# A staging tile of its own for the recurrence's output, and its reload in single 128-row blocks

## Chip, core and metric

One core of a Trainium2 chip runs the whole program. The metric is device microseconds of one execution; the comparison is between medians of several executions. The core has a matrix engine (TensorE), VectorE, ScalarE, GpSimd, the sync engine SP, and 16 DMA engines that all queues share. In the profile they are PE (with PEld for its weight loads), DVE, ACT, POOL and SP; a "q" behind a name (SPq, ACTq) is an instruction of that engine's sequencer, such as the issue of a DMA.

## What is computed

One layer of a hybrid decoder for 1024 tokens of width 1024, in float32. The input is normed and projected by one large matrix; one part of the columns goes to dilated sliding-window attention, one to the RWKV-7 recurrence, one to the gates:

```python
h = rmsnorm(x, norm_mix_pre)
f_att, f_rwkv, f_gate = split(h @ w_in)
o_att  = dilated_window_attention(...)                  # 3 groups, 12 heads
o_rwkv = rwkv7_time_mix(token_shift(f_rwkv), ...)       # 16 heads of 64
gates  = sigmoid(f_gate + b_gate)
merged = gates[0] * (o_att @ w_att_branch) + gates[1] * (o_rwkv @ w_rwkv_branch)
x = x + rmsnorm(merged @ w_out, norm_mix_post)
h = rmsnorm(x, norm_ffn_pre)
x = x + rmsnorm(square(relu(h @ w_ffn1)) @ w_ffn2, norm_ffn_post)
```

The change lies in the recurrence. For every head a 64 x 64 state goes through the tokens; its output y is normed per head, scaled and shifted, given a bonus term and a gate:

```python
state = state*decay + outer(state @ -kk, kk*a) + outer(v, k);  y_t = state @ r_t
y = (y - mean(y)) * rsqrt(var(y) + eps) * ln_w + ln_b
o_rwkv = (y + sum(r*k*r_k) * v) * g           # g = sigmoid(fg) @ w_g2
```

## The kernel before, in words

Every dense product takes both operands in two parts (hi and lo, made by `split_hi_lo`, L40: a cast on ScalarE and a subtraction on VectorE) and adds three matmuls (`mm3`, L203; lines L209, L211, L213). Weights come through a ring of raw tiles (`Weights`, L152). After the input norm, `Project` makes the recurrence's operands and writes them to HBM; attention follows, with the inverses of the chunk matrices beside it; then comes the stage of this change, and after it the merge, the output projection and the feed-forward part.

The recurrence (`Chain`, L817) takes the 1024 tokens in 16 chunks of 64. For each chunk `load` (L840) brings operands U, SV, TB and BKT from HBM into tiles with two buffers, SV being the state with the values. `chunk` (L858) issues five groups of 32 small matmuls, named here by their outputs and lines: pr (L874), py (L879), a second pr (L883), pst (L889), py (L896). Between them stand copies and sums: RS (L876, VectorE) after the first pr, the two halves of SV (L884 on ScalarE and L885 on VectorE) after the second, the next chunk's state (L893, VectorE) after pst, and yt (L898, ScalarE) after py. pst reads both halves of SV.

After each second chunk, a block J of 128 tokens is complete and `norm` (L901) runs on it: mean (L914 to L916, VectorE), then Square into the scratch tile y2 (L918, ScalarE), the sum over y2 (L920, VectorE), a power on GpSimd (L923), and the scaling and bonus (L924 to L926). Later `post` (L929) multiplies by the gate (matmul L937, VectorE L938) and transposes the block in two halves of four (L948, TensorE). For blocks 0 to 5 ScalarE copies the halves into a tile (L953) and issues a store of 512 KB to the HBM tensor O_d (L956). That tile is allocated under the name y2 in a pool with one buffer, so it is the norm's scratch tile again. Blocks 6 and 7 go straight to the operands of the next product (`direct`, L951).

Those operands are ohi and olo, which hold the recurrence's output for the branch projection as eight row blocks of 128 rows by 1024 tokens. They are allocated where the normed hidden states hhi and hlo lay, once the last dense step on these is issued. `load_branch` (L984) fills them from O_d through the tile orw with two buffers: one call for tokens 0 to 511, one for tokens 512 to 767 (blocks 4 and 5), each in four pieces of two row blocks. `Merge.first` (L1005) then starts the branch projection on the first 512 tokens, and on the next 256, for two output tiles, going through all eight row blocks for each.

The order of work: for TensorE and GpSimd it is the order of the program text, which `weave` (L62) makes by planned costs and due times. In this stage the main line is gate and attention branch projections (`gt.open`, `gt.branch`), and the chunks and the posts are woven in as sides. For ScalarE, VectorE and SP a scheduler orders the instructions by a simulated timeline before the program is built, with the chunks' steps at high priority. On the chip each engine, and SP's queue of DMA issues, works in its order; a wait holds up what stands behind it. The pools reuse memory, and a new tile waits until the last reader of the old one is done, a store's DMA included.

Of the kernel before, what the change touches and what calls it, by code (L numbers as in the profile page):

```python
# [9 lines left out]
F32 = mybir.dt.float32  # L10
# [29 lines left out]
def split_hi_lo(nc, raw, hi, lo):  # L40
    nc.scalar.copy(hi, raw)  # L41
    nc.vector.tensor_sub(lo, raw, hi)  # L42
# [774 lines left out]
class Chain:  # L817
# [111 lines left out]
    def post(self, J):  # L929

        g, nc, one = self.g, self.g.nc, self.one
        ts = slice(J * 128, (J + 1) * 128)
        sf, yf, ready = self.normed.pop(J)
        yield 0.0, max(0.0, ready - g.clock)
        for cs in HALF:
            pg = self.ps.tile([128, 512], F32, name="po")
            nc.tensor.matmul(pg, sf, self.wg[:, cs], start=True, stop=True)  # L937
            nc.vector.tensor_mul(yf[:, cs], yf[:, cs], pg)  # L938
            yield 858.0, 1200.0
        direct = self.direct is not None  # L940
        if not direct:
            self.split = J + 1
            oT = one.tile([128, 8, 128], F32, name="y2")
        for q in range(2):
            pt = self.ps.tile([128, 512], F32, name="po")
            for i in range(4):
                k = q * 4 + i
                nc.tensor.transpose(pt[:, i * 128:(i + 1) * 128], yf[:, k * 128:(k + 1) * 128], g.ident)  # L948
            p3, ks = pt.rearrange("p (k t) -> p k t", k=4), slice(q * 4, q * 4 + 4)
            if direct:  # L950
                split_hi_lo(nc, p3, self.direct[0][:, ks, ts], self.direct[1][:, ks, ts])  # L951
            else:
                nc.scalar.copy(oT[:, ks, :], p3)  # L953
            yield 430.0, 1500.0
        if not direct:
            nc.scalar.dma_start(g.O_d[:, :, ts], oT)  # L956
# [27 lines left out]
def load_branch(g, wk, ohi, olo, j0, j1):  # L984

    nc, ts = g.nc, slice(j0 * 128, j1 * 128)
    for q in range(4) if j1 > j0 else ():
        ks = slice(q * 2, q * 2 + 2)
        orw = wk.tile([128, 2, 512], F32, name="orw")[:, :, 0:(j1 - j0) * 128]
        nc.sync.dma_start(orw, g.O_d[:, ks, ts])  # L990
        split_hi_lo(nc, orw, ohi[:, ks, ts], olo[:, ks, ts])

# [456 lines left out]
def layer(tc, ins, out):  # L1449
# [4 lines left out]
    with ExitStack() as c:  # L1454
# [46 lines left out]
        with ExitStack() as c1:  # L1501
# [39 lines left out]
            with ExitStack() as c2:  # L1541
                ch = Chain(g, ins, c2)
                run, posts = Side(ch.run(), 1.1), Side(ch.posts())
                step = lambda f, ci: f(ci, gp) if f == gt.open else f(ci, at.hi, at.lo)
                weave(g, seq(*[step(*x) for x in order[1:-2]]), rest=(run, posts))
                hs.close()
                with tc.using_default_side("left"):
                    op = pool(os, "op")
                    owk = pool(os, "owk", bufs=2)
                ohi = op.tile([128, 8, 1024], F32R, name="ohi")  # L1550
                olo = op.tile([128, 8, 1024], F32R, name="olo")
                ch.direct = (ohi, olo)
                mg = Merge(g, W, ohi, olo)
                done = ch.posted
                load_branch(g, owk, ohi, olo, 0, min(done, 4))
                load_branch(g, owk, ohi, olo, 4, done)

                def ready():
                    if ch.posted < 6:
                        return False  # L1560
                    load_branch(g, owk, ohi, olo, done, ch.split)
                    return True

                weave(g, seq(*[step(*x) for x in order[-2:]], mg.first(ready)), run, posts)
# [87 lines left out]
```

## Time and profile before

| | us |
|---|---|
| median of 3 runs | 1954.45 |
| lowest, highest | 1944.74, 1958.83 |
| the profiled execution, its own time | 1958.2 |
| its span in the profile | 1956.5 |

Mean granted TensorE clock of the profiled execution: 0.972 of full speed. Busy times over the span:

| engine | busy us | share |
|---|---|---|
| PE | 1850.8 | 95% |
| DVE | 1230.8 | 63% |
| ACT | 793.7 | 41% |
| POOL | 307.4 | 16% |

Times inside the profile are counted from the start of the span. A matmul counts as busy from its start to a modelled end, at whatever clock it runs, so a busy PE may still be slow. In timelines a bracket behind a row gives the idle time before it on that engine and what ended it. The name y stands for y2 (numbers behind names are left out), so "O_d<-y" is the store of L956.

### The profile page before, as it was taken

To read this page: it belongs to the slowest core of one execution; us is meant where nothing else is said; L and a number is where in the kernel's file an instruction comes from. 1 tells how busy PE (TensorE), PEld (TensorE's weight loads), DVE (VectorE), ACT (ScalarE), POOL (GpSimd) and SP (SyncE) were. 2 spreads that over 40 slices of the span, in tenths; PEclk is the share of its full clock that TensorE was granted. 3 is DMA by queue.
4 is the path that set the end of the run, shared out by engine and by line. 5 is a ranking of instruction groups with operands and counts; after the bars stand their busy time and mean duration, and the time that the engine had idled before them with its cause. 6 is when DMAs were issued, how large, how long until landed. Compare 5 with 4: busy or idle time off the path is not lost.

```text
span 1956.5 us, 30888 instructions
## 1 busy us (share of the span) xinstructions
PE 1850.8 (95%) x12183; PEld 1509.2 (77%) x12183; DVE 1230.8 (63%) x1857; ACT 793.7 (41%) x1379; POOL 307.4 (16%) x398
## 2 busy tenths in 40 slices
PE   8999999999999999978888899989999998999996
PEld 7888888887787887666666788767888887888885
DVE  6777777734324324436566654668777776776877
ACT  7533333323534525312222333336666655433342
POOL 2011111126141507013333300310000000000001
PEclk9999999999998999989998999999999999999998
DMA  6355556652242241399898454436454447453225
GB/s 181 92 138 139 148 151 153 153 136 69 52 141 55 69 103 40 82 240 235 209 221 208 141 197 136 148 112 229 141 162 143 153 153 241 144 187 136 87 98 182
DMA packets 324914, 283.83 MB, mean 145 GB/s; under 512 B 84926, under 2 KB 275488, under 8 KB 324384
## 3 DMA queue, kind: packets, MB, share of 16 engines
q1 hardware_dynamic: 261984, 247.76, 44.5%
q10 hardware_dynamic: 60672, 26.75, 5.1%
q0 software_dynamic: 2112, 7.34, 1.1%
q8 instruction: 96, 1.57, 0.3%
q14 instruction: 50, 0.41, 0.1%
HBM read 184.70 MB, written 96.57 MB: 144 GB/s over the span
## 4 chain that ended last, share of the span: by engine, by line
PE 76%; DMA 9%; DVE 5%; issue 4%; POOL 3%; ACT 2%; SPq 1%; ACTq 0%; DVEq 0%; POOLq 0%
PE fx L1400 16%; PE fx L1252 14%; PE pd L209 12%; PE pd L211 12%; PE pd L213 12%; DMA O_d<-y 3%; DMA SV<-V_d 2%; PE pm L460 2%; DMA U<-AK_d 1%; PE pm L430 1%; PE po L694 1%; POOL X L515 1%; SPq L501 1%; POOL tmp L514 1%; PE ppt L679 1%
## 5 line engine op out<-in xcount | busy, mean ns | idle before, releaser
L1400 PE MATMUL fx<-w2s,x 128*128 128x512 f32 (+1 forms) x1362 | 307.8, 388 | 5.9 <-DVE w2s L42 4.1
L209 PE MATMUL pd<-hhi,whi 128*128 128x512 f32 (+1 forms) x880 | 300.9, 419 | 0.4 <-DVE Q L590 0.4
L1400 PEld LDWEIGHTS fx<-w2s,x 128*128 128x128 f32 x1362 | 254.9, 189 | 59.0 <-DVE w2s L42 4.4
L211 PE MATMUL pd<-hlo,whi 128*128 128x512 f32 (+1 forms) x880 | 276.9, 392 | 1.0 <-DVE mv L125 1.0
L213 PE MATMUL pd<-hhi,wlo 128*128 128x512 f32 (+1 forms) x880 | 276.0, 391 | 0.0
L42 DVE TENSOR_TENSOR wlo<-raw,whi 128x512 fp32r<-128x512 f32 (+2 forms) x164 | 113.5, 726 | 169.9 <-ACT whi L41 167.4
L211 PEld LDWEIGHTS pd<-hlo,whi 128*128 128x128 f32 x880 | 167.6, 190 | 37.0 <-DVE mv L125 1.3
L213 PEld LDWEIGHTS pd<-hhi,wlo 128*128 128x128 f32 x880 | 167.8, 191 | 35.9
L1252 PE MATMUL fx<-xh,wop 128*128 128x512 f32 x600 | 187.7, 390 | 2.6 <-ACT e L1256 1.6
L209 PEld LDWEIGHTS pd<-hhi,whi 128*128 128x128 f32 x880 | 152.4, 191 | 33.3 <-issue 8.6
L41 ACT CAST whi<-raw 128x512 fp32r<-128x512 f32 (+2 forms) x164 | 92.2, 608 | 198.2 <-PE pd L211 147.4
L1252 PEld LDWEIGHTS fx<-xh,wop 128*128 128x128 f32 x600 | 112.6, 188 | 27.1 <-ACT e L1256 2.0
L41 ACT CAST x<-xr 128x1024 fp32r<-128x1024 f32 x56 | 59.0, 1054 | 153.2 <-issue 87.0
L1252 PE MATMUL fx<-xl,wop 128*128 128x512 f32 x300 | 116.8, 389 | 0.0
L42 DVE TENSOR_TENSOR x<-xr,x 128x1024 fp32r<-128x1024 f32 x56 | 68.4, 1222 | 62.4 <-ACT x L41 62.4
L1354 POOL TENSOR_TENSOR rs<-mv,nhalf 128x1 f32<-128x1 f32 x8 | 6.3, 789 | 629.1 <-ACT jk L1365 608.7
L1181 ACT ACTIVATE e<-e 128x512 f32<-128x512 f32 x128 | 80.2, 633 | 31.0 <-DVE e L1276 10.5
L1252 PE MATMUL fx<-mh,wop 128*128 128x512 f32 x240 | 78.1, 395 | 0.2 <-ACT e L1213 0.2
L666 DVE CUSTOM_DVE_ANT_0 sc<-psc,bias 128x128 f32<-128x128 f32 (+1 forms) x96 | 30.1, 348 | 68.5 <-PE psc L661 52.4
L471 ACT COPY BKs<-pm 128x512 f32<-128x512 f32 x32 | 18.8, 588 | 131.0 <-PE pm L469 107.6
L515 POOL TENSOR_TENSOR X<-X,tmp 128x30 f32<-128x30 f32 (+14 forms) x120 | 65.8, 548 | 9.4
L451 POOL TENSOR_TENSOR BKg<-BK,GC 128x512 f32<-128x512 f32 x32 | 38.6, 1206 | 179.8 <-PE pm L469 175.7
(301 smaller groups left out, 3522.3 us busy)
## 6 DMA issues: line engine op xcount, KB each, us to landing
raw<-in_w_in SPq DMA_DIRECT2D x60, 512.0 KB, 4.3
S_d<-e SPq DMA_DIRECT2D x112, 256.0 KB, 2.1
xr<-S_d SPq DMA_DIRECT2D x56, 512.0 KB, 3.4
raw<-in_w_ffn SPq DMA_DIRECT2D x32, 512.0 KB, 5.1
w<-in_w_ffn SPq DMA_DIRECT2D x16, 1024.0 KB, 5.7
xt<-in_x SPq DMA_DIRECT2D x16, 512.0 KB, 5.5
AR_d<-AR SPq DMA_DIRECT2D x8, 1024.0 KB, 7.3
BKT_d<-BKs ACTq DMA_DIRECT2D x32, 256.0 KB, 3.4
```

The lines of the kernel that those rows point to most:

```text
L41: nc.scalar.copy(hi, raw)
L42: nc.vector.tensor_sub(lo, raw, hi)
L209: nc.tensor.matmul(o, whi[k], xh[k], start=(k == 0), stop=False)
L211: nc.tensor.matmul(o, whi[k], xl[k], start=False, stop=False)
L213: nc.tensor.matmul(o, wlo[k], xh[k], start=False, stop=(k == kt - 1))
L451: nc.gpsimd.tensor_mul(t, BK[:, csls[b], :], g.GC[:, m, csls[b]].unsqueeze(2).to_broadcast([128, 4, 128]))
L460: nc.tensor.matmul(pair[hp][:, i * 128:(i + 1) * 128], BK[side[hp], cc, :], AR[side[hp], cc, :], start=True, stop=True)
L515: nc.gpsimd.tensor_add(X[:, s + 1:32, 0:s], X[:, s + 1:32, 0:s], tv)
L666: nc.vector.tensor_tensor_reduce(out=sc[:, c0:256], in0=pair[hp][:, c0:256], in1=bias[:, h, c0:256], scale=1.0, scalar=3.0e38, op0=ALU.add ...
L1181: self.g.nc.scalar.activation(t, t, f)
L1252: nc.tensor.matmul(out, op[:, w, k, :], xop[v][:, k, :], start=(n == 0 and not add), stop=(n == 11), skip_group_check=add)
L1400: nc.tensor.matmul(po[:, cols], x[:, xi, ts], w[:, wi, cols], start=(first and m == 0), stop=(last and m == 2), skip_group_check=more)
```

## The change

The staging tile of `post` gets a name of its own, oT, in the same pool with one buffer, 4 KB in each partition. `load_branch` goes by single row blocks: eight loads per call instead of four, each half as large, through an orw tile of half the size (two buffers of 2 KB instead of 4 KB in each partition).

```diff
@@ Chain.post
         if not direct:
             self.split = J + 1
-            oT = one.tile([128, 8, 128], F32, name="y2")
+            oT = one.tile([128, 8, 128], F32, name="oT")
@@ load_branch
-    for q in range(4) if j1 > j0 else ():
-        ks = slice(q * 2, q * 2 + 2)
-        orw = wk.tile([128, 2, 512], F32, name="orw")[:, :, 0:(j1 - j0) * 128]
+    for k in range(8) if j1 > j0 else ():
+        ks = slice(k, k + 1)
+        orw = wk.tile([128, 1, 512], F32, name="orw")[:, :, 0:(j1 - j0) * 128]
         nc.sync.dma_start(orw, g.O_d[:, ks, ts])
         split_hi_lo(nc, orw, ohi[:, ks, ts], olo[:, ks, ts])
```

## Rows read from the trace of the kernel before

**Rows 1.** The page's part 4: chain that ended last, shares by engine.

```profile
PE 76%; DMA 9%; DVE 5%; issue 4%; POOL 3%; ACT 2%; SPq 1%; ACTq 0%; DVEq 0%; POOLq 0%
```

**Rows 2.** Waits of ACT, 915 to 1090 us: total us, times, longest.

```profile
ACT y L918 <- DMA O_d<-y: 36.4, 4, 11.7
...
ACT y L953 <- DMA O_d<-y: 10.4, 1, 10.4
```

**Rows 3.** Waits of PE, 975 to 1090 us.

```profile
PE pst L889 <- ACT SV L884: 11.0, 4, 4.6
PE pst L889 <- DVE SV L885: 3.9, 4, 1.4
```

**Rows 4.** Timeline of all engines, 1002 to 1016 us: start, length, what.

```profile
1002.42 0.52 ACTq L956 DMA_DIRECT2D O_d<-y  x1
...
1011.15 1.06 ACT L918 ACTIVATE y<-yt 128x1024 f32<-128x1024 f32 x1 [8.77 <-DMA O_d<-y]
...
1014.24 1.97 PE L889 MATMUL pst<-SV,BKT 128*64 128x64 f32 x30 [1.04 <-DVE SV L885]
```

**Rows 5.** Windows: length; busy PE, PEld, DVE, ACT, POOL; PEclk, DMA share, GB/s.

```profile
971.00:1002.00 31.00, 27.86 (x386) 21.45 (x386) 20.27 (x27) 7.72 (x15) 10.60 (x5) 1.00 0.92 223
1002.00:1036.00 34.00, 30.55 (x389) 23.61 (x387) 22.74 (x26) 8.54 (x15) 15.04 (x6) 0.90 0.97 240
1036.00:1073.00 37.00, 30.56 (x415) 24.11 (x415) 23.84 (x28) 7.94 (x14) 8.88 (x5) 0.86 0.73 190
```

**Rows 6.** Timeline of PE: where each chunk's pr group (L874) starts, 942 to 1090 us.

```profile
942.47 1.95 PE L874 MATMUL pr<-SV,U 128*64 128x64 f32 x32
...
954.81 0.33 PE L874 MATMUL pr<-SV,U 128*64 128x64 f32 x2
...
971.14 1.15 PE L874 MATMUL pr<-SV,U 128*64 128x64 f32 x32
...
985.91 0.33 PE L874 MATMUL pr<-SV,U 128*64 128x64 f32 x2
...
1002.46 1.15 PE L874 MATMUL pr<-SV,U 128*64 128x64 f32 x32
...
1020.23 1.15 PE L874 MATMUL pr<-SV,U 128*64 128x64 f32 x32
...
1036.05 1.15 PE L874 MATMUL pr<-SV,U 128*64 128x64 f32 x32
...
1057.19 1.15 PE L874 MATMUL pr<-SV,U 128*64 128x64 f32 x32
...
1071.05 1.15 PE L874 MATMUL pr<-SV,U 128*64 128x64 f32 x32
1072.13 0.66 PE L948 MATMUL po<-ident,yt 128*128 128x128 f32 x4
...
1089.58 1.15 PE L874 MATMUL pr<-SV,U 128*64 128x64 f32 x32
```

**Rows 7.** Tile orw: ns min/median/max of one, first and last start us, forms.

```profile
L41 ACT CAST ohi<-orw x8: 619/828/1047, 1094.3 to 1116.3; 128x1024 fp32r<-128x1024 f32 x4, 128x512 fp32r<-128x512 f32 x4
```

**Rows 8.** Timeline of SP, 825 to 1140 us: the reload's last four issues.

```profile
1104.30 0.36 SPq L990 DMA_DIRECT2D orw<-O_d  x1
...
1106.63 2.69 SPq L990 DMA_DIRECT2D orw<-O_d  x2
...
1111.98 0.53 SPq L990 DMA_DIRECT2D orw<-O_d  x1
```

**Rows 9.** DMA issues, 825 to 1140 us: count, KB each, median us to landing.

```profile
orw<-O_d SPq DMA_DIRECT2D x4, 512.0 KB, 4.9
...
orw<-O_d SPq DMA_DIRECT2D x4, 256.0 KB, 3.4
```

**Rows 10.** Timeline of PE, 1116 to 1126 us: the reloaded blocks, the gate product.

```profile
1119.05 0.28 PE L209 MATMUL pd<-ohi,whi 128*128 128x256 f32 x1
...
1124.40 1.35 PE L937 MATMUL po<-wg,sf 128*128 128x512 f32 x2 [2.54 <-DVE yt L938]
```

## The prediction, made before the change was run

> **What bounds the kernel now.** I read the page's chain of waits first, then waits by engine, then timelines of the stretch that they point to, and the DMA views last. The chain [rows 1] is three quarters TensorE, so what counts is what makes TensorE stand still or run slowly. In the recurrence's stretch, about 838 to 1135 us, TensorE's order is written out by hand: each chunk's five small products lie between steps of the dense projections, so a chunk product that waits holds up the dense steps behind it. ScalarE's waits [rows 2] show the wait that the change touches: the norm's Square (L918) waits 36.4 us in four waits for the store O_d<-y, since its scratch y2 is also the tile from which the block before is stored. A second such wait, 10.4 us, belongs to the staging copy (L953).
>
> ScalarE's idle time costs nothing by itself. What reaches TensorE is in its own waits [rows 3]: the pst product (L889) waits 11.0 us in four waits for ScalarE's copy L884, and 3.9 us in four for VectorE's copy L885. One instance [rows 4]: the store is issued at 1002.42, Square can start only at 1011.15, and pst's last 30 products start at 1014.24. L884 stands behind Square on ScalarE, and L885 behind the reduction (L920) that reads Square's output on VectorE; so two queues carry one store's landing to TensorE. That pst group then takes 1.97 us, where a clean group of the kind takes 1.15 [rows 6], and the granted clock falls to 0.90 and 0.86 of 2.4 GHz in the two stretches that hold the long waits, from 1.00 in the one before [rows 5]: after standing still TensorE runs partly at its 1.2 GHz level.
>
> **Part 1: staging in oT.** Square's and L920's own times stay; only the wait goes. I size it by chunk periods, from one first pr product to the next [rows 6]. The stretch 942.47 to 954.81 holds a Square too, but the store had landed: 12.3 us, of which 0.8 us is a pr group at the lower clock (1.95 against 1.15), so 11.5 clean, with four dense steps. The stretches with a late store, from the rows' starts: 971.14 to 985.91 is 14.8; 1002.46 to 1020.23 is 17.8; 1036.05 to 1057.19 is 21.1; 1071.05 to 1089.58 is 18.5. The first three have four dense steps each. The last has one more and four transposes (0.66 us): a step is (11.5 - 5 x 1.15) / 4 = 1.4, so its clean length is about 13.5. Over 11.5, 11.5, 11.5 and 13.5 they are long by 3.3, 6.3, 9.6 and 5.0 us: sum 24 us. Bounds: 14.9 us, the idle time alone [rows 3], if the slow clock had another reason; 24 us.
>
> What is late next? oT has one buffer, so the staging copy of block J+1 waits for the store of block J. A block is two periods, 28 us and more, and Square's longest wait for a store is 11.7 us [rows 2], so that wait is covered, except for the first pair: its 10.4 us stays as it is.
>
> The next limit is the loads of the coming chunk. In the three stretches 971 to 1073 the DMA engines are busy 0.92 x 31 + 0.97 x 34 + 0.73 x 37 = 88.5 of 102 us [rows 5]. That leaves 13.5 us idle, while I want to take 19.2 out of them (3.3 + 6.3 + 9.6). If the packets' time can't shrink, 5.7 us come back as waits of pr for SV. Against it: 0.5 MB less is loaded there (the two reloads that fit early are half as large), some 2 us at 240 GB/s. Bounds 0 and 6, nearest to these rows: I take 4.
>
> **Part 2: the reload by single blocks.** Bytes are unchanged. Twice four loads become twice eight: SP issues eight more, ScalarE eight more casts, VectorE eight more subtractions. A cast of 1024 columns takes 1047 ns and of 512 619 ns [rows 7], so a split one costs 0.19 us more: 1.5 us for all eight, and I take as much for VectorE. Both engines wait for loads there, so this lies beside.
>
> The two buffers matter more. Hardly any load can run ahead: the destination ohi takes the place of the hidden states, so the first cast is at 1094.3 [rows 7], when the last dense step has read them. Both buffers are full by then. They held four of the first set's eight blocks; now they hold two, and fourteen loads follow instead of six. A buffer goes round by load, cast, subtraction and next issue. In the trace one buffer's loads are issued at 1104.30 and about 1108.96 (the end of the merged pair, less its 0.36), the other's at 1106.63 and 1111.98 [rows 8]: 4.7 and 5.4 us, mean 5.0, for 256 KB. The new first-set loads are of that size. The second set's are 128 KB: by landing times, 4.9 us for 512 KB and 3.4 for 256 KB [rows 9], a line gives 2.65, so 0.75 us off the round and some tenths off a shorter cast and subtraction: I take 4.4 us, between 3.65 and 5.4.
>
> Now count. First reissue at 1095.6 (1094.3, 0.62 and 0.7 us). One buffer takes blocks 2, 4, 6 at 5.0 us each and is free at 1110.6; then second-set blocks 0, 2, 4, 6 at 4.4, so block 6 is issued at 1123.8, block 7 about 0.7 later, and it is split at 1128.9. TensorE reads block 7 of the second set at 1119.05 [rows 10]. It would stand about 10 us. Of that the wait of 2.5 us before the last block's gate product (1124.40) is absorbed, since the norm before it is then no longer late: 7 us net. Bounds: 4 us with rounds of 3.65; 15 us with rounds of 5.4 throughout and nothing absorbed.
>
> The Trainium skill ("DMA: Bandwidth & Descriptors", Anatomy of one DMA) speaks against this part: a transfer has a fixed part of about 2.0 us whatever its size, so halving it halves little. The trace agrees, as 2 x 3.4 - 4.9 gives 1.9 us. By the page alone eight more loads over two buffers would cost an estimated 8 us in place of my 10, and the sum would be some 2 us better.
>
> **Sum.** 24 - 4 - 7 = 13 us less than the profiled execution's own 1958.2, so 1945.2. That execution lies 3.75 us above the median of the three, 1954.45; the forecast against the median is 1954.45 - 13 = 1941.5.
>
> **Rivals** (times against the median).
> - *The reload is hidden* (chance 0.26). Its loads run closer than I count, or TensorE comes to them later, behind the last chunk. Then 24 - 4 = 20, up to 24: 1930 to 1935. For it: the trace's one wait at the gate product is the norm's, not the reload's [rows 10].
> - *DMA becomes the bound* (0.14). The stall moves from pst to pr waiting for SV. With 6 us back and the idle bound of 14.9, then the reload's 7: 2 us gained, 1952.5. For it: shares of 0.92 and 0.97. Against it: 0.73 in the third stretch, where most is gained.
> - *Slower: the two buffers go out of step* (0.11). Place: the fourteen late loads on SP's in-order queue, with casts in ScalarE's order and subtractions in VectorE's. Those also carry the last chunk's yt copy and the last norm, so a cast that waits for its block delays that norm too. If loads no longer overlap, 14 x 4.7 us from 1095.6 end at 1161, 42 us after the need; less 20 that is 22 us slower, 1976. It turns the sign when the pace passes (1119 + 20 - 1095.6) / 14 = 3.1 us a load; I forecast 2.4. For it: on one buffer 5.4 us were seen. Against it: the two buffers' loads do overlap in the trace.
> - *The wait only changes place* (0.03): oT's copy waits where Square did. Then nothing but the reload's cost is left, 1961. Against it: the 28 us between stores.
>
> **How the numbers follow.** The forecast has 0.46. Its own range is 1934 to 1951 (gain 24 - 0 - 4, and 14.9 - 4 - 7). The range for 8 in 10 reaches up to 1957, which takes in the DMA case and most of a costly reload (14.9 - 4 - 15 gives 1959), and down to 1929 for the hidden reload; beyond lie the slower case, most of the wait that changes place, and the tails. One per cent, about what a measurement tells from no change here, is 19.5 us. Faster by more: three quarters of the hidden-reload case and a tenth of the forecast's, 0.25. Slower by more: most of the out-of-step case and little else, 0.10. Within: 0.65.
>
> **What would show it.** Right: ScalarE's wait of Square for O_d is gone; pst's waits for L884 and L885 drop from 14.9 to under 3 us; the chunk periods with a Square and four dense steps last about 11.5 us; the granted clock stays near 1.00 between 971 and 1070; sixteen orw loads, the last fourteen 2 to 3 us apart; a wait of TensorE for ohi or olo of 5 to 10 us before the last gate product, and the time after it unchanged. Wrong: pr waits for SV by more than 5 us in those periods (DMA rival); no wait on the reload (hidden); loads 3 us or more apart and the last norm late (slower).

## The result, and the profile after

| | median, us | runs |
|---|---|---|
| before | 1958.83 (1944.74 to 1971.78) | 15 |
| after | 1942.47 (1936.32 to 1956.14) | 15 |

The ratio is 0.9933, with a 95% interval of 0.9912 to 0.9953: some 13 us less, between 9 and 17. (The two medians lie 16.4 us apart; their ratio, 0.9916, is inside that interval.) The profiled execution of the changed kernel took 1949.08 us, 6.6 above its median, with a span of 1947.4.

The wait that the change aimed at is gone. ScalarE's waits in the changed kernel, 840 to 1140 us:

```profile
ACT y L918 <- DVE yt L916: 25.7, 6, 12.5
ACT ohi L41 <- DMA orw<-O_d: 19.9, 10, 3.8
...
ACT oT L953 <- DMA O_d<-oT: 12.9, 1, 12.9
```

Square (L918) now waits only for its own input. The third row is the wait that one oT buffer keeps, the second block's staging copy for the first block's store, as [rows 2] had it with 10.4 us; the second row has grown from 7.7 us. TensorE's waits of the changed kernel, 945 to 1095 us, answer to [rows 3]:

```profile
PE pr L874 <- DVE SV L893: 4.2, 5, 3.0
PE po L948 <- DVE yt L938: 2.2, 1, 2.2
PE pr L883 <- DVE RS L876: 1.3, 1, 1.3
```

There is no wait of pst for SV any more, where it was 14.9 us. What is left waits for VectorE, none of it for a load. The windows, to be read like [rows 5]:

```profile
958.00:989.00 31.00, 27.91 (x394) 21.41 (x388) 23.63 (x27) 9.31 (x16) 9.93 (x4) 1.00 1.02 240
989.00:1019.00 30.00, 29.33 (x388) 22.48 (x388) 17.92 (x23) 7.87 (x12) 9.52 (x4) 0.94 0.81 204
1019.00:1048.00 29.00, 27.34 (x386) 21.16 (x386) 22.09 (x26) 6.36 (x12) 9.87 (x4) 1.00 1.07 261
1048.00:1075.00 27.00, 27.00 (x386) 21.08 (x386) 19.21 (x27) 8.02 (x14) 9.54 (x4) 1.00 0.88 227
```

The granted clock is 1.00 but for one stretch, and the DMA engines' share (the column before the last) passes 1 in two of them without TensorE waiting for a load. TensorE's timeline, the starts of pr for each chunk from the seventh on (before: [rows 6]), and behind them the first product on the reloaded blocks and the last transposes of the stage:

```profile
946.57 1.15 PE L874 MATMUL pr<-SV,U 128*64 128x64 f32 x32
...
974.45 1.15 PE L874 MATMUL pr<-SV,U 128*64 128x64 f32 x32
...
989.04 0.33 PE L874 MATMUL pr<-SV,U 128*64 128x64 f32 x2 [2.96 <-DVE SV L893]
...
1007.05 1.15 PE L874 MATMUL pr<-SV,U 128*64 128x64 f32 x32
...
1018.88 0.33 PE L874 MATMUL pr<-SV,U 128*64 128x64 f32 x2 [0.24 <-DVE SV L893]
...
1035.38 1.15 PE L874 MATMUL pr<-SV,U 128*64 128x64 f32 x32
...
1048.10 1.15 PE L874 MATMUL pr<-SV,U 128*64 128x64 f32 x32
...
1061.95 1.15 PE L874 MATMUL pr<-SV,U 128*64 128x64 f32 x32
...
1075.45 1.15 PE L874 MATMUL pr<-SV,U 128*64 128x64 f32 x32
...
1094.76 0.39 PE L209 MATMUL pd<-ohi,whi 128*128 128x512 f32 x1
...
1115.46 1.84 PE L937 MATMUL po<-wg,sf 128*128 128x512 f32 x2
...
1122.86 0.66 PE L948 MATMUL po<-ident,yt 128*128 128x128 f32 x4 [1.40 <-DVE olo L42]
```

The last three of these rows in the kernel before:

```profile
1105.64 0.39 PE L209 MATMUL pd<-ohi,whi 128*128 128x512 f32 x1
...
1119.41 1.02 PE L937 MATMUL po<-wg,sf 128*128 128x512 f32 x2
...
1130.35 0.66 PE L948 MATMUL po<-ident,yt 128*128 128x128 f32 x4 [1.40 <-DVE olo L42]
```

The four stretches that were too long took 14.8, 17.8, 21.1 and 18.5 us. Now they take 14.6 (974.45 to 989.04), 11.8 (1007.05 to 1018.88), 12.7 (1035.38 to 1048.10) and 13.5 (1061.95 to 1075.45). From the seventh chunk's pr to the sixteenth's it is 1075.45 - 946.57 = 128.9 us, against 1089.58 - 942.47 = 147.1: 18.2 less. From there to the last transposes it is 47.4 us; before, these started at 1130.35, so it was 40.8: 6.6 more. The spans of the two profiled executions differ by less than these two add up to, 9.1 us (1956.5 and 1947.4): the seventh chunk starts 4.1 us later in the changed one, and the rest of the program is 1.6 us shorter. The reload, in the rows of tile orw and SP's timeline of the changed kernel:

```profile
L41 ACT CAST ohi<-orw x16: 404/508/627, 1080.2 to 1113.9; 128x512 fp32r<-128x512 f32 x8, 128x256 fp32r<-128x256 f32 x8
L42 DVE TENSOR_TENSOR olo<-orw,ohi x16: 411/683/2832, 1080.8 to 1114.4; 128x512 fp32r<-128x512 f32 x8, 128x256 fp32r<-128x256 f32 x8
```

```profile
1082.36 7.07 SPq L990 DMA_DIRECT2D orw<-O_d  x4
...
1092.77 2.31 SPq L990 DMA_DIRECT2D orw<-O_d  x2
...
1099.53 12.65 SPq L990 DMA_DIRECT2D orw<-O_d  x8
```

Fourteen loads are issued after the first cast, and from that cast to the last subtraction's end it is 1114.8 - 1080.2 = 34.6 us. Before it was 23.3, from 1094.3 to 1117.6, the end of the last subtraction in this row of the kernel before:

```profile
L42 DVE TENSOR_TENSOR olo<-orw,ohi x8: 680/954/2327, 1095.3 to 1116.9; 128x1024 fp32r<-128x1024 f32 x4, 128x512 fp32r<-128x512 f32 x4
```

The loads land sooner than I had drawn from [rows 9]; DMA issues of the changed kernel, the last column being us to landing:

```profile
orw<-O_d SPq DMA_DIRECT2D x8, 256.0 KB, 2.7
...
orw<-O_d SPq DMA_DIRECT2D x8, 128.0 KB, 2.2
```

### The profile page after: what moved, and what is told of

It reads as the page before. It is cut to its first block, busy times and chain, and to the rows that moved or that the text cites. A ratio compares the mean times of both kernels' runs of the same rounds, so it can differ in the third digit from the quotient of the medians.

```text
span 1947.4 us, 30913 instructions
## 1 busy us (share of the span) xinstructions
PE 1847.3 (95%) x12183; PEld 1505.6 (77%) x12183; DVE 1232.3 (63%) x1865; ACT 795.9 (41%) x1387; POOL 304.9 (16%) x398
## 4 chain that ended last, share of the span: by engine, by line
PE 80%; DMA 8%; DVE 4%; issue 3%; POOL 2%; ACT 2%; ACTq 0%; SPq 0%; DVEq 0%; POOLq 0%
PE fx L1400 16%; PE fx L1252 14%; PE pd L209 14%; PE pd L211 13%; PE pd L213 12%; DMA U<-AK_d 2%; PE pm L460 2%; PE po L694 1%; PE pm L430 1%; DMA orw<-O_d 1%; POOL X L515 1%; PE ppt L679 1%; DMA O_d<-oT 1%; POOL tmp L514 1%; PE pm L469 1%
## 5 line engine op out<-in xcount | busy, mean ns | idle before, releaser
L471 ACT COPY BKs<-pm 128x512 f32<-128x512 f32 x32 | 18.8, 588 | 132.2 <-PE pm L469 102.4
```

## The experiments

Each kernel was timed against the kernel before on the same chip. "Chunks" is the time from the seventh chunk's pr to the sixteenth's, "end" from there to the start of the last transposes, "reload" from the first cast on orw to the last subtraction's end, each from the kernel's own timeline as above. "Start" is the seventh chunk's pr. The stretches are those of one profiled execution per kernel; "start" lies anywhere between 934 and 947, so one kernel's start alone shows little.

| kernel | ratio to before, 95% | start | chunks | end | reload |
|---|---|---|---|---|---|
| before | 1 | 942.5 | 147.1 | 40.8 | 23.3 |
| after | 0.9933 [0.9912, 0.9953] | 946.6 | 128.9 | 47.4 | 34.6 |
| own tile, old reload | 0.9920 [0.9890, 0.9951] | 941.4 | 128.8 | 42.0 | 24.6 |
| reload only | 1.0022 [0.9997, 1.0047] | 938.7 | 142.9 | 47.9 | 33.8 |
| one wait back | 1.0005 [0.9978, 1.0032] | 946.3 | 138.1 | 50.7 | 34.8 |
| packed second call | 0.9931 [0.9904, 0.9957] | 945.6 | 127.6 | 45.4 | 31.8 |
| four single buffers | 0.9902 [0.9867, 0.9936] | 936.6 | 128.9 | 44.7 | 24.3 |
| one single buffer | 1.0057 [1.0030, 1.0084] | 946.8 | 129.5 | 71.7 | 57.7 |
| no bonus on GpSimd | 0.9914 [0.9886, 0.9942] | 941.7 | 127.0 | 47.4 | 33.7 |
| own tile, old reload, first store | 0.9876 [0.9839, 0.9913] | 935.7 | 130.0 | 41.9 | 24.6 |
| three buffers, first store | 0.9902 [0.9874, 0.9930] | 934.4 | 130.6 | 43.8 | 24.5 |
| first store only | 0.9901 [0.9867, 0.9935] | 936.0 | 129.2 | 47.6 | 34.7 |
| bonus on VectorE | 1.0043 [1.0021, 1.0065] | 941.6 | 149.4 | 45.1 | 25.1 |

**Each part alone.** First the tile without the new reload, on the kernel before:

```diff
-            oT = one.tile([128, 8, 128], F32, name="y2")
+            oT = one.tile([128, 8, 128], F32, name="oT")
-        RS = self.two.tile([128, 8, 64], F32, name="RS")
+        RS = self.two.tile([128, 8, 64], F32, name="RS", bufs=1)
-        sf = two.tile([128, 128], F32, name="sf")
+        sf = two.tile([128, 128], F32, name="sf", bufs=1)
```

> The staging tile alone: oT as in the change, the reload as before (four loads per call through the larger orw). The memory for both is found by giving RS and sf one buffer instead of two. My theory: the store's wait is worth some 17 to 20 us at TensorE and the reload gives back 6 to 7 of it in the change, so without the new reload the ratio to the kernel before is about 0.990 (18 to 20 us less). Rival, the reload costs nothing: the ratio of the change itself, 0.993. Rival, DMA is the next bound: also about 0.993, with pr waiting for U or SV by 5 us and more after 940 us.

The ratio was 0.9920. Its interval holds both 0.990 and the change's 0.993, so the times don't decide; the stretches do. "Chunks" is that of the change to 0.1 us, "end" is 42.0 in place of 47.4. Its rows of tile orw:

```profile
L41 ACT CAST ohi<-orw x8: 619/830/1052, 1075.6 to 1098.9; 128x1024 fp32r<-128x1024 f32 x4, 128x512 fp32r<-128x512 f32 x4
L42 DVE TENSOR_TENSOR olo<-orw,ohi x8: 681/956/2794, 1076.6 to 1099.5; 128x1024 fp32r<-128x1024 f32 x4, 128x512 fp32r<-128x512 f32 x4
```

Then the reload without the tile, on the changed kernel:

```diff
-            oT = one.tile([128, 8, 128], F32, name="oT")
+            oT = one.tile([128, 8, 128], F32, name="y2")
```

> The reload by single blocks alone: staging stays in y2, so Square waits for the store as before. My theory: the reload's fourteen late loads cost 6 to 7 us, ratio to the kernel before 1.003 to 1.004, with Square's four waits for O_d back (about 36 us on ScalarE) and 14 to 15 us of TensorE's waits at pst. Rival, the reload is hidden: 1.000. Rival, the gain came from a shift of memory or order and not from the wait: below 1.000.

1.0022, with the expected 1.003 inside the interval and 1 just as well; what is excluded is that the gain came from the new reload or its smaller buffers. The end is 7.1 us longer than before. In its waits of TensorE, 840 to 1140 us, those of [rows 3] are back (in this window the kernel before has 11.0 and 5.3 us):

```profile
PE pst L889 <- ACT SV L884: 8.5, 4, 3.0
...
PE pst L889 <- DVE SV L885: 6.1, 6, 1.4
```

So the two parts are near what the prediction had. The tile takes 18 us off the chunks with the old reload (147.1 to 128.8) and 14 with the new one (142.9 to 128.9), as the four stretches with a late store take 67.0 us in this execution and 72.2 in that of the kernel before. The reload adds 5 to 7 us to the end (42.0 to 47.4, 40.8 to 47.9). That it is the wait and not the place of the new tile in memory, the next kernel shows: it has the new tile too.

**One wait put back.**

```diff
-            oT = one.tile([128, 8, 128], F32, name="oT")
+            oT = one.tile([128, 8, 128], F32, name="y2" if J == 4 else "oT")
```

> The change, but block 4 is staged in y2 again, so that one Square (that of block 5) waits for a store. In the kernel before that one's stretch was 9.6 us too long. My theory: this one wait is worth 6 to 10 us, ratio to the kernel before about 0.9975, and the chunk period that held 12.7 us in the changed kernel is 18 to 22. Rival, DMA is the next bound, so that a wait only lets the loads catch up: 0.994, two thirds of it given back in the next two periods.

The timelines of this kernel show the wait and the stretch around it:

```profile
1032.58 1.15 PE L874 MATMUL pr<-SV,U 128*64 128x64 f32 x32
...
1055.45 1.15 PE L874 MATMUL pr<-SV,U 128*64 128x64 f32 x32
```

```profile
1045.94 1.06 ACT L918 ACTIVATE y<-yt 128x1024 f32<-128x1024 f32 x1 [13.43 <-DMA O_d<-y]
```

A wait of 13.4 us on ScalarE makes the stretch 22.9 us in place of 12.7, and the chunks 9.2 us longer: nothing is given back behind it. The stretch is longer than the 18 to 22 I expected, and the ratio, 1.0005, is above the 0.9975: 14 us worse than the change's, more than those 9, though the two intervals leave room for 9. In the trace another 3.3 us lie in the end. Of these 2.3 come before the reload starts: the first cast on orw stands 7.0 us behind the sixteenth chunk's pr and not 4.7, as two of TensorE's steps there take 2.08 and 1.84 us where they take 1.13 and 1.03 in the change.

**What in the reload costs time.** The reload could be slow because there are more loads, or because fewer bytes are held. Three experiments turn on that, and one of the kernels further down. In the first, the second call fills a buffer with two row blocks of 256 tokens:

```diff
-    for k in range(8) if j1 > j0 else ():
-        ks = slice(k, k + 1)
-        orw = wk.tile([128, 1, 512], F32, name="orw")[:, :, 0:(j1 - j0) * 128]
+    w = (j1 - j0) * 128
+    n = 512 // w if w else 8
+    for k in range(0, 8, n) if w else ():
+        ks = slice(k, k + n)
+        orw = wk.tile([128, 512], F32, name="orw")[:, 0:n * w].rearrange("p (k t) -> p k t", k=n)
```

> The change, but the second call of the reload puts two row blocks of 256 tokens into one orw buffer of the same size: four loads of 256 KB there instead of eight of 128 KB, twelve in all. My theory: the second set's loads set the end of the reload, and it ends 4 to 7 us earlier; 2 to 4 us of it reach the end of the stage, ratio to the kernel before 0.991 to 0.992. Rival, the reload is hidden or the last norm sets the end: 0.993, as the change.

The reload is 2.8 us shorter than in the change, not 4 to 7, and the end 2.0, the low side of what I expected; the ratio doesn't show it and is the rival's 0.993. In the second, four buffers of one block each:

```diff
-                    owk = pool(os, "owk", bufs=2)
+                    owk = pool(os, "owk", bufs=4)
```

(and RS and sf with one buffer, as above).

> The change with four orw buffers instead of two (room from RS and sf with one buffer each), so the reload goes by sixteen single-block loads but holds as many bytes as in the kernel before. It tells what costs time in the reload: too few bytes in flight, or the number of loads. My theory, bytes in flight: from the first cast on orw to the last subtraction 22 to 26 us (34.6 in the change, 23.4 before), and from the last chunk's pr to the last transposes 41 to 43 us as before, not 47; ratio to the kernel before 0.990 to 0.992. Rival, each load's fixed part: twelve late loads at the change's 2.3 us still take 28 to 30 us, and the stage's end gives back 4 us of the 6.6.

```profile
L41 ACT CAST ohi<-orw x16: 399/508/622, 1070.2 to 1093.7; 128x512 fp32r<-128x512 f32 x8, 128x256 fp32r<-128x256 f32 x8
L42 DVE TENSOR_TENSOR olo<-orw,ohi x16: 421/554/2834, 1070.9 to 1094.1; 128x512 fp32r<-128x512 f32 x8, 128x256 fp32r<-128x256 f32 x8
```

Sixteen loads, and the reload takes 24.3 us like the kernel before's eight. The number of loads costs next to nothing; the bytes in flight decide, that is, how often the set of buffers has to be filled for all the rows. With four fills the kernels of the table take 23.3 to 25.1 us, with six (packed) 31.8, with eight (as in the change) 33.7 to 34.8, with sixteen (below) 57.7. The end, 44.7 us, came down less than the reload and less than the 41 to 43 I expected: the last gate product then waits 3.3 us for the last norm. In the third, one buffer:

```diff
-                    owk = pool(os, "owk", bufs=2)
+                    owk = pool(os, "owk", bufs=1)
```

> The change with one orw buffer instead of two: the slower rival's case made real, in which no two reloads overlap. My theory: fifteen late loads at 4.4 to 5.0 us a round, some 70 us from the first cast to the last subtraction instead of 34.6; TensorE stands for the difference, 33 to 38 us more than in the change, ratio to the kernel before 1.010 to 1.013. Rival, the reload is mostly hidden behind the last chunk and norm: under 15 us more, ratio below 1.001.

```profile
L41 ACT CAST ohi<-orw x16: 404/508/620, 1081.7 to 1138.6; 128x512 fp32r<-128x512 f32 x8, 128x256 fp32r<-128x256 f32 x8
L42 DVE TENSOR_TENSOR olo<-orw,ohi x16: 424/556/1653, 1082.4 to 1139.0; 128x512 fp32r<-128x512 f32 x8, 128x256 fp32r<-128x256 f32 x8
```

Fifteen late loads take 55.3 us from the first reissue (1084.06) to 1139.4, 3.7 us a round, not the 4.4 to 5.0 of my estimate, as the loads land faster. The reload is 23 us longer than in the change, the end is 24, and the ratio 0.0124 or 24 us higher: at this length the whole of it reaches the end of the stage. The prediction's slower rival is thereby priced. At 2.3 us a load (1082.36 to 1114.8, fourteen loads) the change is 13 us faster than before, at 3.7 it is 11 slower; on a straight line between these two points, an estimate, the sign turns at 3.1.

**GpSimd and VectorE.** The changed kernel without the two products on vt, so the bonus factor and the norm's bias are left out:

```diff
-        nc.gpsimd.tensor_mul(vt, vt, g.BON[:, J, :].unsqueeze(2).to_broadcast([128, 16, 64]))
-        nc.gpsimd.tensor_add(vt, vt, self.lnb.rearrange("p (h i) -> p h i", i=64))
```

> The change without GpSimd's two products on vt (L909, L910): the bonus factor and the norm's bias are left out, the values are added as loaded. In the changed kernel VectorE's operations that start while these run last up to 2 us longer, and TensorE then waits for RS, for SV and for yt. My theory: those stretches go, VectorE's L869 has a mean near 0.7 us instead of 1.15, the reload's first subtractions take 0.7 us each instead of 4.3 for two, and the time is 4 to 6 us below the change, ratio to the kernel before 0.990 to 0.992. Rival, VectorE's long operations have another cause (its own queue): L869 keeps its mean, and the ratio is that of the change, 0.993.

VectorE's groups, 838 to 1135 us, in this kernel (its lines are two lower from there on):

```profile
L869 DVE TENSOR_TENSOR stG<-SV,GC 64x512 f32<-64x512 f32 x32 | 24.0, 749 | 0.7
```

In the changed kernel it was

```profile
L869 DVE TENSOR_TENSOR stG<-SV,GC 64x512 f32<-64x512 f32 x30 | 28.5, 951 | 0.7
```

and before 1146 ns (the 1.15 us of my expectation is the kernel before's). So GpSimd's products are what lengthens it. L893, which takes one of its inputs from TensorE's output pst, has a mean of 688 ns in all three. The chunks are 1.9 us shorter; the end is not, although its first subtractions no longer take 4.3 us for two. The ratio's interval overlaps that of the change: shown as a mechanism, not as a gain.

**The one wait that is left.** Block 1 alone is staged in y2, where Square hardly meets its store (it waits 0.8 us for it in the first kernel below and not at all in the second):

```diff
-            oT = one.tile([128, 8, 128], F32, name="oT")
+            oT = one.tile([128, 8, 128], F32, name="y2" if J == 1 else "oT")
```

on the changed kernel:

> The change as it is, with block 1 alone staged in y2, nothing else. It prices the one wait that oT with one buffer keeps. My theory: TensorE's 4 to 6 us at L948 go and the time is 3 to 6 us below the change, ratio to the kernel before 0.990 to 0.992. Rival, the loads are the bound in the first six chunks: 0.993, with 3 us and more of added waits of pr for U or SV there.

and on the own tile with the old reload:

> The own staging tile with the reload as before (RS and sf with one buffer), and block 1 alone staged in y2, so that it need not wait for block 0's store, the one wait that oT with one buffer keeps (2 to 7 us at TensorE in the runs so far). My theory: TensorE's wait at the transposes L948 for the staging copy goes, no Square waits for block 1's store, 3 to 6 us less than the own tile alone; ratio to the kernel before 0.988 to 0.990. Rival, the loads of the first six chunks are the bound there and the wait only lets them catch up: 0.992, with more waiting of pr for U or SV in the chunk behind it.

In both, TensorE's wait for the staging copy is gone and "start" comes at 936, where the change's was 946.6 in its one profiled execution. The ratios are 0.9901 and 0.9876. The first seems 6 us below the change, the second 9 us below the own tile alone, but each pair of intervals overlaps. Nor does the early start settle it: the kernel with four single buffers starts at 936.6 as well, and it keeps that wait, though it costs TensorE only 0.4 us there (5.7 in the change, 2.0 in the own tile alone). So what this wait is worth stays open. Waits of pr for U and SV did not grow: 14.6 us in the first before 945, 16.7 in the change. The second has the lowest ratio of the study, 24 us below the kernel before (17 to 32), though its interval overlaps those of several others. It pays for sf's single buffer, in its waits of TensorE:

```profile
PE po L937 <- DMA sf<-SF_d: 4.2, 1, 4.2
```

So I put the parts together with three buffers of one block, packed, sf with two buffers, RS with one:

> A version to beat both kernels: the change, with three orw buffers (room from RS with one buffer; sf keeps two), the second call in pairs of row blocks (twelve loads in all), and block 1 alone staged in y2. My theory: reload from the first cast to the last subtraction 24 to 27 us, no wait of TensorE for a staging copy, no wait of the gate product for sf; ratio to the kernel before 0.986 to 0.988. Rival, two parts of it share one slack (the last norm sets the end as soon as the reload is quick): 0.990, as with four buffers.

0.9902, short of the 0.986 to 0.988 I expected: the reload is quick, 24.5 us with four fills in twelve loads, and the rival of the one slack holds. Its rows of tile orw, and the wait of TensorE that shows who sets the end now:

```profile
L41 ACT CAST ohi<-orw x12: 608/620/622, 1069.6 to 1092.8; 128x512 fp32r<-128x512 f32 x12
L42 DVE TENSOR_TENSOR olo<-orw,ohi x12: 675/684/2833, 1070.2 to 1093.4; 128x512 fp32r<-128x512 f32 x12
```

```profile
PE po L937 <- DVE yt L938: 4.1, 1, 4.1
```

This is the last norm. Last, the products on vt moved to VectorE in that kernel, `nc.gpsimd` to `nc.vector` in the two lines above:

> The version with three buffers, but the two products on vt (L909, L910) are issued on VectorE instead of GpSimd. VectorE has 2.4 us more work per block; in exchange nothing of GpSimd but one product (L924) can lengthen VectorE's operations. My theory: L869's mean falls towards 0.75 us, but the products then stand in VectorE's order and wait there for the load of vt; no gain, ratio within 0.003 of the three-buffer version. Rival, the lengthening is what is left to gain: 3 to 5 us below it.

A miss in size: 1.0043, some 28 us slower than the same kernel with the products on GpSimd, 18.8 of them in the chunks. L869's mean did fall, to 779 ns. VectorE's waits of this kernel tell why:

```profile
DVE vt L909 <- DMA vt<-V_d: 40.3, 8, 9.0
```

The products stand in VectorE's order and wait there for their load, 5 us in each block, with the copies for pst behind them: pst waits 13.8 us for L885 again. It is the wait for the store over again, on another engine and for another transfer.

## Why the prediction came out right

The forecast was 13 us less; the ratio gives 13 (9 to 17). The mechanism of both parts held. That the sum came out to the microsecond is partly luck: two terms were wrong inside and made good by others.

- *The store's wait reaches TensorE through two queues.* Right. No pst wait is left, and the change's chunks are as short as those of the own tile alone. The single wait put back costs 9.2 us in the chunks, with 6.7 us of pst waiting for L884 again; the prediction had 9.6 for that one.
- *24 us, less 4 for the loads.* 20 forecast, 18.2 in the trace. The size held, the cause of the deduction did not: no pr waits for a load after 945 us, at a DMA share up to 1.07. What came in its place is VectorE: the first stretch kept 14.6 us, 2.96 of it a wait for L893. That stood behind operations lengthened by GpSimd, two small subtractions among them that took 2.15 us together beside GpSimd's L924 (two such take 0.49 at 1079.48). The stretch behind it, at a granted clock of 0.91, took 18.0 us where it had been 16.6. That this cost was as large as the 4 us for loads is luck. A DMA share near 1 did not mean that TensorE waited for loads.
- *oT's one buffer.* Right: only the first pair of blocks meets, with 12.9 us on ScalarE and 5.7 on TensorE. I had booked it as unchanged (10.4 and 5.1 before). What it is worth isn't shown: the times of the first-store kernels overlap with those of their partners.
- *The reload.* Right in size. Fourteen late loads, 34.6 us from the first cast to the last subtraction, where my count went from 1094.3 to 1128.9, also 34.6. The rounds behind it were off in a way that cancelled, which is luck: landings were 2.7 and 2.2 us, not 3.4 and 2.65, while the first buffer came free late, at 1082.36, since two subtractions took 4.3 us. My 4.4 us for a small round doesn't even follow from its own terms: 5.0 less 0.75 less some tenths is about 4.0.
- *What of it reaches the end.* The reload became 11.3 us longer. In the change the last transposes start 8.1 us after its last subtraction, before 12.8, when the last norm was late too: 4.7 us are absorbed, and 6.6 remain; forecast 7. The other kernels fit this: wherever the reload is slow (six fills and more), the last transposes start 8 to 9.4 us after it, elsewhere 11.9 to 15.7. My sign for it failed in size: TensorE's waits for ohi and olo are 3.0 us, not 5 to 10. The gate product comes 20.7 us after the first ohi product where it was 13.8, also because the granted clock was 0.87 in this stretch and had been 1.00.
- *Its cause.* The Trainium skill ("DMA: Bandwidth & Descriptors", Anatomy of one DMA) gives a transfer a fixed part of about 2.0 us, in a section on DMAs that GpSimd issues. SP issues those of this reload, and the trace agrees in size: 2 x 2.2 - 2.7 is 1.7 us. But eight more of them cost nothing where four buffers were open; a fixed part counts here only by the loads that wait for each other.
- *The rivals.* The hidden reload falls with the end stretches, 47.4 against 42.0 us. DMA as the bound falls with TensorE's waits. The slower case is real, and lies at one buffer: its turning point, 3.1 us a load, agrees with the estimate from the runs.

## What to carry to other kernels

A scratch tile that doubles as the source of a store ties the next use of the scratch to that store's landing, and an in-order queue hands this wait to everything behind it: look for an operation that waits on a store of something it doesn't read, and give the staging its own tile. When the memory for it comes out of a reload's buffers, count the bytes in flight over the round of load, cast and release (how often the buffers must be filled), not the number of loads; and look whether another tile with two buffers needs only one.

## What was not expected

VectorE's operations on two inputs in SBUF, the on-chip memory of the tiles, can stand still while GpSimd runs one of its own. In the changed kernel, VectorE's and then GpSimd's timeline:

```profile
975.25 3.37 DVE L916 TENSOR_TENSOR yt<-yt,mu 128x1024 f32<-128x1024 f32 x1
```

```profile
975.15 2.39 POOL L910 TENSOR_TENSOR vt<-vt,lnb 128x1024 f32<-128x1024 f32 x1
```

L916 takes 1.22 us elsewhere. Here it ends 1.08 us after GpSimd's operation does, as if it had begun then; the recorded 3.37 us are mostly waiting. The Trainium skill ("SBUF — State Buffer", SBUF: two separate sides) says this for a VectorE operation with two SBUF inputs beside a GpSimd operation that reads SBUF: they share a port pair that the first to start keeps for its whole instruction, and the other is blocked. The trace agrees: GpSimd's operation started first, by 0.10 us, and without GpSimd's products on vt L869 comes down to 749 ns.
